# A hybrid decoder layer: the conditioning tiles beside the projections of four heads instead of six

## The chip, the cores and the metric

The kernel runs on one core of one Trainium2 chip. The metric is the device time of one execution in microseconds (us); it stands beside the span, which is the time between the first and the last instruction that the profiler recorded.

## The reference

One layer, 512 tokens of width 2048, all in float32. A conditioning vector `c` gives six vectors of 2048 (shift, scale and gate for the mixing and for the MLP) by a product with `w_ada` (2048 x 12288, 100 MB). The mixing has 8 heads of HGRN2 and 8 heads of Gated DeltaNet in parallel, each with four projections of 128 columns of `w_in`.

```
c_act = silu(c)
mod = c_act @ w_ada + b_ada
sh_m, sc_m, gt_m, sh_f, sc_f, gt_f = split(mod, 6)
h = rmsnorm(x, pre_mix_norm) * (1 + sc_m) + sh_m
proj = h @ w_in
o = concat(hgrn2_group(proj[:4096]), gdn_group(proj[4096:]))
x = x + gt_m * rmsnorm(o @ w_out, post_mix_norm)
h = rmsnorm(x, pre_ffn_norm) * (1 + sc_f) + sh_f
x = x + gt_f * rmsnorm(square(relu(h @ w_ff1)) @ w_ff2, post_ffn_norm)
```

`w_in` is 2048 x 8208; a row takes 32,832 bytes, a row of `w_ada` 49,152.

## The kernel before

Activations stand with the feature dimension on the partitions: `hH` and `hL` are the 16 tiles of `h`, split into a rounded part and a rest so that three fast products of rounded numbers give the accuracy of float32. Every weight tile is split the same way.

**Weights.** `WeightStream` walks a list `plan` of weight tiles, each `raw` tile 128 partitions x 1024 floats (512 KB). One fetch (`get`) of tile *i* first issues the load of tile *i*+3 on SyncE's queue (L66), then splits tile *i*+1: ScalarE casts it to `wh` (L81), VectorE subtracts to `wl` (L83). There are three `raw` buffers, two `wh` and two `wl`. SyncE works in order: a load whose buffer isn't free holds back every load behind it.

**Projections.** A start stage (to 294 us in the profile) computes shift and scale of the mixing, `h`, and the projections of heads zero and one. Then a loop over heads two to seven projects each head's eight blocks of 128 columns (four of each group). A block is two tiles, `("in1", column, half)`, so a head has 16 fetches and the loop 96. A tile is read as 1024 pieces of 128 floats, one from each of 1024 rows of `w_in`. The products go to `pj` in PSUM, 24 matmuls per fetch. In the trace the tiles of a head are `raw32` to `raw47` for head two, and so on to `raw96` to `raw111` for head six and `raw112` to `raw127` for head seven. (The profile leaves the numbers out and writes `raw`; all of them are issued at L66.)

**Recurrences.** Between these matmuls stand those of the recurrences of the heads before (names like `p`, `pa`, `po`). Which matmul stands where is set when the program is written, by a clock of modelled costs; TensorE's and SyncE's order is then fixed. ScalarE, VectorE and GpSimd get their order from a scheduler. All engines work in order.

**The conditioning of later stages.** The three segments that are wanted after the mixing (scale and shift of the MLP, gate of the mixing: segments 4, 3 and 2 of `w_ada`, in this order) are computed beside the projections of heads two to seven, by the generator `ada_rest`. A segment has 4 column blocks of 512, a block 16 rows per partition: 3 x 4 x 16 = 192 steps. A step is one load of 128 x 512 floats (256 KB, `ada`, L302), issued six steps ahead into seven buffers; one scaling on ScalarE by an element of `c` per partition (L320), which is placed behind the last cast of a weight tile; and one add on GpSimd into the block's accumulator `aacc` (L322). Five steps after a block's last step follows its end: for segments 4 and 3 sums over the partitions on TensorE (`pca`); for segment 2 a load of a row of `b_ada` (`bgt`, L1151) and an add of it on GpSimd (L1152). After the projections those four accumulators are summed on TensorE (`pgw`) and multiplied with `post_mix_norm` (`wpost`, L1287).

Each fetch calls `on_get`, which runs as many steps as are due: after *n* fetches of the loop, 192 *n* / `total` steps. What is left of the generator after the last projection is run then (`for _ in steps: pass`).

The output projection (`pout`), the residual and norms, and the MLP (`pf`, `pg`) follow; the MLP takes more than half of the span.

Of the kernel before, what the change touches and what calls it, by code (L numbers as in the profile page):

```python
# [15 lines left out]
P = 128  # L16
# [92 lines left out]
def hybrid_layer_kernel(  # L109
# [30 lines left out]
    def wrow(W, r, nb):  # L140
        return W[r : r + 256, nb * 512 : (nb + 1) * 512].rearrange("(k p) n -> p k n", p=P)
# [14 lines left out]
    plan = []  # L156
# [15 lines left out]
    for nbs in ((0,), (0, 1), (2,), (3,)):  # L172
        for i, r in enumerate(OUT_PAIRS):
            for nb in nbs:
                e = (("out", r, nb), wrow(Wo, r * P, nb))
# [1005 lines left out]

    steps = ada_rest()
    pace = {"on": False, "n": 0, "done": 0}
    total = sum(1 for e in plan if e[0][0] == "in1") - 12

    def on_get():
        if not pace["on"]:
            return
        pace["n"] += 1
        while pace["done"] * total < pace["n"] * 192:  # L1190
            pace["done"] += 1
            next(steps, None)
# [130 lines left out]
    with ExitStack() as st:  # L1323
# [42 lines left out]
        for nb in range(1, 4):  # L1366
            ps4 = [bank("pj", f"pout{nb}_{tok}") for tok in range(3)] + [bank("sg", f"pout{nb}_3")]
            n = 8 if nb < 3 else 8 - NLAST
# [25 lines left out]
        for kt in range(KT):  # L1394
# [10 lines left out]
            if kt % 3 < 2:  # L1405
                nc.scalar.activation(out=h2H[:, kt, :], in_=ht, func=AF.Identity, bias=shf[:, kt : kt + 1])
                nc.vector.scalar_tensor_tensor(out=h2L[:, kt, :], in0=ht, scalar=shf[:, kt : kt + 1],
                                               in1=h2H[:, kt, :].bitcast(F32), op0=ALU.add, op1=ALU.subtract)
# [188 lines left out]
```

## Time and profile before

| | us |
|---|---|
| median of 3 runs | 2716.35 |
| lowest, highest | 2715.49, 2717.22 |
| the profiled execution | 2714.78 |
| its span | 2713.1 |
| busy: TensorE (PE) | 2563.6 |
| busy: VectorE (DVE) | 1440.6 |
| busy: ScalarE (ACT) | 1016.4 |
| busy: GpSimd (POOL) | 569.9 |
| projections of heads two to seven, first and last `pj` matmul | 294 to 1096 |

The page of the profile gives the busy time of each engine, the span in 40 slices (a digit is a busy share in tenths; PEclk is the granted clock of TensorE in tenths), the DMA queues, and groups of instructions. Other views are tables of time windows (per engine the busy time and, in brackets, the number of instructions, then granted clock, busy share of the 16 DMA engines and GB/s), waits (who waited for whom: us in total, times, longest), and one tile's instructions (shortest / median / longest in ns, first and last start). SPq is SyncE's queue. In the DMA view of a window, a row of a load has the number issued, the size of one and the median us from issue to landing. "Busy" of TensorE is a time in which matmuls are in flight, not a measure of its rate.

### The profile page before, as it was taken

How to read it: one execution, taken by the hardware profiler on the slowest of the kernel's cores; microseconds unless marked ns; L12 is line 12 of the kernel's file. 1: busy time of each engine (PE TensorE's matmuls, PEld its weight loads, DVE VectorE, ACT ScalarE, POOL GpSimd, SP SyncE). 2: the span in 40 equal slices, each digit the busy share in tenths (PEclk: the TensorE clock that was granted, in tenths of full speed). 3: DMA queues.
4: the chain of work that ended last, by engine and by line, in shares of the span. 5: the costliest groups of instructions: out<-in, count | busy, mean ns of one | idle time of the engine just before them, and what ended most of it. 6: DMA issues, size and time to landing. Idle time of an engine off the chain costs nothing.

```text
span 2713.1 us, 34048 instructions
## 1 busy us (share of the span) xinstructions
PE 2563.6 (94%) x12987; PEld 2080.2 (77%) x12987; DVE 1440.6 (53%) x2265; ACT 1016.4 (37%) x1675; POOL 569.9 (21%) x496
## 2 busy tenths in 40 slices
PE   5889999999997789999999999999999999999997
PEld 3667777777775567788788888888888888888886
DVE  7997868776865366634533343334333344334346
ACT  5543554454543242433533233332233223322233
POOL 4560344544444340000100000000000000000003
PEclk8999999999998899999999999999999999999999
DMA  9974885778899985445233333333333333332342
GB/s 280 283 186 73 133 138 128 151 138 153 139 138 103 98 135 79 143 129 186 90 117 109 118 112 115 111 114 111 112 117 111 115 110 116 105 101 93 101 171 109
DMA packets 335938, 350.65 MB, mean 129 GB/s; under 512 B 17191, under 2 KB 255001, under 8 KB 334621
## 3 DMA queue, kind: packets, MB, share of 16 engines
q1 hardware_dynamic: 335578, 348.42, 53.8%
q8 instruction: 102, 1.67, 0.2%
q14 instruction: 62, 0.51, 0.1%
q10 hardware_dynamic: 196, 0.06, 0.0%
HBM read 340.01 MB, written 8.40 MB: 128 GB/s over the span
## 4 chain that ended last, share of the span: by engine, by line
PE 65%; DVE 5%; DMA 3%; issue 2%; POOL 1%; ACT 1%; SPq 0%; DVEq 0%; ACTq 0%; POOLq 0%
PE pf L203 25%; PE pg L203 25%; PE pj L203 7%; PE pout L203 6%; DMA raw<-in_w_in_dram 2%; DVE wl L83 1%; PE pa L203 1%; POOL y L1521 0%; POOL aacc L322 0%; DVE x2r L1539 0%; DVE uc L912 0%; DVE utmp L910 0%; PE p L203 0%; DVE zkT L364 0%; PE pz L203 0%
## 5 line engine op out<-in xcount | busy, mean ns | idle before, releaser
L83 DVE TENSOR_TENSOR wl<-raw,wh 128x1024 fp32r<-128x1024 f32 x418 | 525.4, 1258 | 827.3 <-ACT wh L81 821.0
L81 ACT CAST wh<-raw 128x1024 fp32r<-128x1024 f32 x424 | 445.9, 1052 | 1216.5 <-PE pg L203 477.9
L203 PE MATMUL pf<-h2L,wh 128*128 128x512 f32 x1024 | 399.2, 390 | 0.0
L203 PE MATMUL pf<-h2H,wh 128*128 128x512 f32 x1024 | 399.2, 390 | 0.0
L203 PE MATMUL pf<-h2H,wl 128*128 128x512 f32 x1024 | 398.9, 390 | 0.0
L203 PE MATMUL pg<-wh,gL 128*128 128x512 f32 x992 | 385.9, 389 | 0.0
L203 PE MATMUL pg<-wl,gH 128*128 128x512 f32 x992 | 385.9, 389 | 0.0
L203 PE MATMUL pg<-wh,gH 128*128 128x512 f32 x992 | 385.9, 389 | 0.0
L203 PE MATMUL pj<-hH,wh 128*128 128x512 f32 x768 | 328.9, 428 | 7.3 <-ACT wh L81 7.3
L322 POOL TENSOR_TENSOR aacc<-ada,aacc 128x512 f32<-128x512 f32 x180 | 268.5, 1492 | 256.7 <-ACT ada L320 222.7
L203 PE MATMUL pj<-hH,wl 128*128 128x512 f32 x768 | 308.2, 401 | 6.9 <-DVE wl L83 6.9
L203 PE MATMUL pj<-hL,wh 128*128 128x512 f32 x768 | 306.7, 399 | 0.0
L322 POOL TENSOR_TENSOR gacc<-ada,gacc 128x512 f32<-128x512 f32 x64 | 83.2, 1300 | 940.6 <-ACT ada L320 940.6
L203 PEld LDWEIGHTS pf<-h2L,wh 128*128 128x128 f32 x1024 | 192.5, 188 | 39.9
L203 PEld LDWEIGHTS pf<-h2H,wh 128*128 128x128 f32 x1024 | 192.5, 188 | 39.8
L203 PEld LDWEIGHTS pf<-h2H,wl 128*128 128x128 f32 x1024 | 192.4, 188 | 39.8
L203 PEld LDWEIGHTS pg<-wl,gH 128*128 128x128 f32 x992 | 186.2, 188 | 38.7
L203 PEld LDWEIGHTS pg<-wh,gH 128*128 128x128 f32 x992 | 186.2, 188 | 38.6
L203 PEld LDWEIGHTS pg<-wh,gL 128*128 128x128 f32 x992 | 186.2, 188 | 38.6
L1482 DVE TENSOR_TENSOR y<-pg,y 128x512 f32<-128x512 f32 x232 | 154.6, 687 | 70.7 <-PE pg L203 70.7
L203 PEld LDWEIGHTS pj<-hH,wl 128*128 128x128 f32 x768 | 148.0, 193 | 44.0 <-DVE wl L83 10.5
L203 PEld LDWEIGHTS pj<-hH,wh 128*128 128x128 f32 x768 | 148.5, 193 | 37.8 <-ACT wh L81 8.7
(411 smaller groups left out, 3346.3 us busy)
## 6 DMA issues: line engine op xcount, KB each, us to landing
raw<-in_w_ff_dram SPq DMA_DIRECT2D x256, 512.0 KB, 3.7
ada<-in_w_ada_dram SPq DMA_DIRECT2D x256, 256.0 KB, 7.9
raw<-in_w_in_dram SPq DMA_DIRECT2D x96, 512.0 KB, 9.4
adas<-in_w_ada_dram SPq DMA_DIRECT2D x128, 256.0 KB, 5.4
raw<-in_w_out_dram SPq DMA_DIRECT2D x40, 512.0 KB, 3.8
raw<-in_w_in_dram SPq DMA_DIRECT2D x40, 256.0 KB, 4.2
raw<-in_w_in_dram SPq DMA_DIRECT2D x48, 128.0 KB, 5.3
xo<-in_x_dram SPq DMA_DIRECT2D x8, 512.0 KB, 8.7
```

The lines of the kernel that those rows point to most:

```text
L81: self.cast = self.nc.scalar.copy(out=h, in_=raw).ins
L83: eng.tensor_tensor(out=lo, in0=raw, in1=h.bitcast(F32), op=ALU.subtract)
L203: nc.tensor.matmul(ps, lhsT=lhsT, rhs=rhs, start=start, stop=stop)
L322: nc.gpsimd.tensor_tensor(out=acc, in0=a, in1=acc, op=ALU.add)
L1482: nc.vector.tensor_tensor(out=dst, in0=ps4[tok], in1=dst, op=ALU.add)
```

## The change

`total`, the number of fetches over which the 192 steps are spread, was the number of `in1` tiles less 12, 84: the steps ran from head two into the fourth fetch of head seven. It becomes the number of tiles of heads two to five, 64. The count of fetches stops at `total`, so the steps that `on_get` runs stop at 192 exactly; the end of the last block of segment 2, which one further call would have run, is now left to the loop after the last projection.

```diff
     steps = ada_rest()
     pace = {"on": False, "n": 0, "done": 0}
-    total = sum(1 for e in plan if e[0][0] == "in1") - 12
+    total = sum(1 for e in plan if e[0][0] == "in1" and e[0][1] % 1024 < 6 * P)
 
     def on_get():
         if not pace["on"]:
             return
-        pace["n"] += 1
+        pace["n"] = min(pace["n"] + 1, total)
         while pace["done"] * total < pace["n"] * 192:
             pace["done"] += 1
             next(steps, None)
```

SyncE's queue, from the third weight tile of head six on. An `ada` name has the first column of its block in `w_ada` and the row of the step: `ada4608_5` is segment 2, second block, row 5; `ada5632` is the fourth and last block. Before:

```order
L66 DMA raw98_7785<-in_w_in_dram 128x8x128
L302 DMA ada4608_5_7791<-in_w_ada_dram 128x512
L302 DMA ada4608_6_7794<-in_w_ada_dram 128x512
L302 DMA ada4608_7_7798<-in_w_ada_dram 128x512
L66 DMA raw99_7877<-in_w_in_dram 128x8x128
L302 DMA ada4608_8_7883<-in_w_ada_dram 128x512
L302 DMA ada4608_9_7887<-in_w_ada_dram 128x512
L1151 DMA bgt0_7891<-in_b_ada_dram 1x512
L66 DMA raw100_7940<-in_w_in_dram 128x8x128
```

Now, the same queue from the second-last tile of head five on (`E6` is a load for head six's recurrence that stands at this place in both):

```order
L66 DMA raw95_7745<-in_w_in_dram 128x8x128
L302 DMA ada5632_9_7751<-in_w_ada_dram 128x512
L1151 DMA bgt2_7755<-in_b_ada_dram 1x512
L302 DMA ada5632_10_7758<-in_w_ada_dram 128x512
L302 DMA ada5632_11_7762<-in_w_ada_dram 128x512
L66 DMA raw96_7809<-in_w_in_dram 128x8x128
L302 DMA ada5632_12_7815<-in_w_ada_dram 128x512
L302 DMA ada5632_13_7819<-in_w_ada_dram 128x512
L302 DMA ada5632_14_7823<-in_w_ada_dram 128x512
L840 DMA E6_7852<-gd_184 128x4x128
L66 DMA raw97_7903<-in_w_in_dram 128x8x128
L302 DMA ada5632_15_7909<-in_w_ada_dram 128x512
```

The last conditioning load now stands before `raw98`; from there to `raw127` the queue holds weight tiles and head seven's `E7` alone. In heads two to five each weight load has three conditioning loads behind it, where it had two or three.

The load of the last row of `b_ada`, `bgt3`, stood between `raw119` and `raw120` of head seven; now it is issued after `raw130`, a tile of `w_out`, right ahead of the four loads of `post_mix_norm`.

ScalarE's queue in head four, at the casts of two weight tiles (`thvT4`, `zvT4`, `upvT4`: the convolution of head four's values). Before:

```order
L81 CAST wh71_6058<-raw71_5899 128x1024
L360 COPY upvT4_6043<-pj6656_5898 128x512
L362 ACTIVATE zvT4_6046<-pj6656_5898,convT_98 128x512
L320 ACTIVATE ada6656_7_5792<-ada6656_7_5792,c2_99 128x512
L320 ACTIVATE ada6656_8_5905<-ada6656_8_5905,c2_99 128x512
L320 ACTIVATE ada6656_9_5909<-ada6656_9_5909,c2_99 128x512
L368 ACTIVATE thvT4_6051<-zvT4_6046 128x512
```

Now:

```order
L81 CAST wh71_6176<-raw71_6030 128x1024
L360 COPY upvT4_6161<-pj6656_6029 128x512
L362 ACTIVATE zvT4_6164<-pj6656_6029,convT_98 128x512
L320 ACTIVATE ada7680_2_6040<-ada7680_2_6040,c2_99 128x512
L320 ACTIVATE ada7680_3_6044<-ada7680_3_6044,c2_99 128x512
L320 ACTIVATE ada7680_4_6085<-ada7680_4_6085,c2_99 128x512
L368 ACTIVATE thvT4_6169<-zvT4_6164 128x512
```

At such a fetch with three steps nothing changes but the step's number (27 steps on); a fetch with two gets a third scaling ahead of the copies behind it.

## The prediction

> **What bounds the kernel now.** I read the page first, for which engine fills the span and where it does not.
>
> ```profile
> span 2713.1 us, 34048 instructions
> PE 2563.6 (94%) x12987; PEld 2080.2 (77%) x12987; DVE 1440.6 (53%) x2265; ACT 1016.4 (37%) x1675; POOL 569.9 (21%) x496
> PE   5889999999997789999999999999999999999997
> PEclk8999999999998899999999999999999999999999
> DMA  9974885778899985445233333333333333332342
> ```
>
> TensorE is the bound nearly everywhere. The exception inside the kernel is slices 13 and 14 (one slice is 67.8 us, so about 814 to 950 us): TensorE falls to seven and eight tenths, its granted clock falls with it, and the DMA engines are at nine. That lies inside the stretch that the change touches, the projections of heads two to seven. So the second view is a table of windows, one per head. The heads' bounds are the starts of their first `pj` matmul; the last two rows cut head seven where the conditioning ends, and the row of 1100 is the output projection.
>
> ```profile
> core 0: us, PE busy (x) PEld busy (x) DVE busy (x) ACT busy (x) POOL busy (x), PEclk, DMA share, GB/s
> 294.00:434.00 140.00, 131.73 (x895) 105.64 (x894) 106.13 (x238) 66.41 (x143) 66.71 (x52) 0.96 0.81 141
> 434.00:564.00 130.00, 122.26 (x832) 97.63 (x832) 96.52 (x187) 60.46 (x125) 62.96 (x49) 0.99 0.68 144
> 564.00:690.00 126.00, 118.57 (x755) 95.94 (x754) 86.29 (x166) 58.25 (x122) 57.98 (x45) 0.99 0.83 150
> 690.00:810.00 120.00, 114.74 (x723) 90.46 (x722) 85.85 (x151) 58.45 (x113) 57.09 (x45) 1.00 0.88 138
> 810.00:984.00 174.00, 130.52 (x700) 101.28 (x698) 80.76 (x154) 58.90 (x115) 56.38 (x46) 0.87 0.99 109
> 984.00:1020.00 36.00, 34.23 (x192) 27.94 (x191) 31.43 (x49) 19.57 (x47) 22.95 (x18) 1.00 0.70 119
> 1020.00:1097.00 77.00, 76.91 (x492) 61.38 (x492) 44.27 (x102) 20.82 (x39) 4.22 (x5) 1.00 0.52 82
> 1100.00:1140.00 40.00, 38.98 (x204) 30.72 (x202) 28.72 (x54) 19.13 (x39) 2.39 (x2) 1.00 0.39 120
> ```
>
> Head six takes 174 us where head five takes 120 and head seven 36 + 77 = 113. Its DMA engines are busy all the time (0.99) and yet move less, 109 GB/s against 138 to 150. So they are the bound there, and something makes their work dearer. The DMA view of that stretch (787 to 960 us, from its loads' first data on) and one row of the waits in it:
>
> ```profile
> q1 hardware_dynamic: 21607, 17.42, 101.1%
> ada<-in_w_ada_dram SPq DMA_DIRECT2D x37, 256.0 KB, 15.7
> raw<-in_w_in_dram SPq DMA_DIRECT2D x16, 512.0 KB, 20.3
> ACT wh L81 <- DMA raw<-in_w_in_dram: 79.0, 12, 10.8
> ```
>
> 16 weight loads and 37 conditioning loads fill 101% of 173 us, 175 us of all 16 engines' time. ScalarE's casts wait 79.0 us for weights; TensorE's own waits carry other names, because ScalarE works in order and its other copies stand behind a cast that waits. What makes the weights dear is not their size, which is that of every head. I take it to belong to head six's loads, for it comes and goes with them. SyncE's issue of a weight load, which grows when the DMA engines don't keep up:
>
> ```profile
> L66 SPq DMA_DIRECT2D raw<-in_w_in_dram x17: 378/379/1979, 661.7 to 782.8; - x17
> L66 SPq DMA_DIRECT2D raw<-in_w_in_dram x16: 1656/3310/4324, 794.2 to 956.4; - x16
> ```
>
> The load issued at 782.8 is `raw96`, head six's first, and the one at 956.4 is `raw112`, head seven's first. From 960 us on the DMA has recovered, while the conditioning goes on:
>
> ```profile
> DMA  9998998894999657985568896547998897888655
> GB/s 70 56 88 132 271 276 195 220 125 96 337 198 152 122 129 236 243 146 68 71 199 226 111 60 110 109 129 263 297 207 119 122 134 78 103 168 173 174 66 48
> ```
>
> (960 to 1010 us in 40 slices, with 11 conditioning loads and 7 weight loads issued.) It is no accident of one execution: 50 us lost once in a while would show between the runs, and they lie within 1.73 us of each other.
>
> **The change part by part.** A conditioning step is one load of 256 KB, one scaling on ScalarE and one add on GpSimd. Before, 84 fetches carry 192 steps, 16/7 each: 64 x 16/7 = 146 steps in heads two to five, 46 in heads six and seven. Now the first 64 fetches carry 3 each. So 46 steps move ahead, 11.5 more per head in heads two to five; nothing is added or removed in number.
>
> *Head six loses its conditioning loads.* Price of one load in engine time: the fastest slice above moves 337 GB/s, so 0.78 us for 256 KB; the output projection's loads, in rows as long, run at 120 / 0.39 = 308 GB/s, 0.85 us. The slow stretch itself never exceeds 217 GB/s in a slice, 1.21 us, but weights move in that slice too. So 37 x 0.78 = 29 us to 37 x 1.21 = 45 us. I take 29, from the slice most nearly of conditioning alone.
>
> ```profile
> GB/s 91 54 150 117 93 156 69 148 81 95 124 45 113 107 69 217 46 109 101 53 195 67 80 93 62 164 84 41 141 72 76 161 81 140 101 122 83 46 113 97
> ```
>
> It counts whole on the path: 174 - 29 = 145 us is still more than the 120 us of head five, so head six remains paced by its weights, 175 - 29 = 146 us over 16, some 9.1 us each.
>
> The Trainium skill, page "DMA: Bandwidth & Descriptors", section "Latency and other measured facts", has a rule on this: when each partition reads at a large power-of-two row pitch, copies fell from 207 GB/s to 103. The pitch of w_ada between partitions is 768 KiB; at 207 GB/s, an estimate from that page, the 37 loads would be worth 47 us instead of 29. The slice of 337 GB/s disagrees, so I keep the row.
>
> *Heads two to five get 46 more steps.* On ScalarE 0.72 us each and on GpSimd 1.49 us, from these rows:
>
> ```profile
> L320 ACT ACTIVATE ada<-ada,c x244: 705/718/732, 299.6 to 2344.8; 128x512 f32<-128x512 f32 x122
> L322 POOL TENSOR_TENSOR aacc<-ada,aacc 128x512 f32<-128x512 f32 x180 | 268.5, 1492 | 256.7 <-ACT ada L320 222.7
> SPq L302 <- POOL aacc L322: 66.9, 46, 7.2
> PE py L203 <- DVE Ud L928: 1.6, 1, 1.6
> ```
>
> Per head that is 8 us on ScalarE (58 to 66 of 120 to 140 now) and 17 us on GpSimd (57 to 67 now): both stay under 65%. It lies beside TensorE, except where a copy for a recurrence stands behind a third scaling instead of a second. TensorE is idle 8.27 + 7.74 + 7.43 + 5.26 = 28.7 us in the four heads now. If all of it came from the 146 steps, 46 more would cost 28.7 x 46 / 146 = 9.0 us, and the stretch without steps (0.09 us idle in 77) speaks for that; the waits that are named there, as the last row above (660 to 790 us), are for VectorE in the recurrences, which speaks for nothing. Ends 0 and 9, I take the middle, 4.5.
>
> *SyncE's queue.* Each fetch issues its weight load and then three conditioning loads; the last waits for GpSimd's add two steps back, and the next weight load stands behind it. The third row above is that wait over 564 to 790 us: 1.5 us each, 7.2 at most, against a weight load that lands three fetches (over 22 us) before its matmuls. Cover: 22 less the landing of 11.1 us below, about 11 us; nothing charged. If it went, each fetch would wait for the excess.
>
> ```profile
> DMA to landing us min/median/max: 8.5/11.1/17.7
> ```
>
> *DMA share in heads two to five.* 11.5 loads x 0.85 = 9.8 us per head: 0.81 becomes 0.88, 0.68 becomes 0.76, 0.83 becomes 0.91, 0.88 becomes 0.96. Below one, so nothing charged; head five is near, see the rivals.
>
> *The bias rows.* Three of four `bgt` loads move with their steps into head five, the fourth to the end of the projections. GpSimd waits for them in order:
>
> ```profile
> POOL aacc L1152 <- DMA bgt<-in_b_ada_dram: 45.2, 3, 24.4
> POOL aacc L1152 <- DMA bgt<-in_b_ada_dram: 2.1, 1, 2.1
> L203 PE MATMUL pgw<-aacc,ones x8: 592/592/595, 1098.1 to 1101.2; 128*128 128x512 f32 x8
> L1287 SPq DMA_DIRECT2D wpost<-in_post_mix_norm_dram x4: 327/375/462, 1085.1 to 1101.1; - x4
> ```
>
> 43.1 us of that wait fell in the slow stretch and 2.1 us (the second row, 980 to 1120 us) after it. In head five I take 2 us in all on the path; ends 0, and 30 if three loads each held TensorE for a 10 us landing. The fourth is issued just ahead of `wpost` at 1085; even at 5.4 us to land (the slowest `wpost`) and 1.3 us for the add it is ready by 1092, 6 us before `pgw` at 1098. Cover: those 6 us; without them the wait's excess would go straight to the output projection.
>
> *The column sums and the order.* The sums of segments four and three come earlier in TensorE's order, the same instructions; no cost.
>
> Sum: -29 + 4.5 + 2 = -22.5 us. The profiled execution took 2714.78 us around its span of 2713.1, and the median of the runs is 1.57 us above it: 2716.35 - 22.5 = 2694 us. A measurement here tells about 0.2%, 5.4 us, from no change.
>
> **The rivals.**
>
> *Head six runs like its neighbours.* If dear weights need the conditioning beside them, head six falls from 174 to 120 us: -54 + 6.5 = -47.5, 2669 us. For it: no head is dear without conditioning beside it. Against: heads three to five have the same mixture and are not dear.
>
> *The dearness goes with segment two's columns of w_ada*, steps 144 to 183, loaded in the same stretch. They would then be in head five: 37 / 3 = 12.3 fetches at 175 / 16 + 0.7 x 0.85 = 11.5 us each instead of 7.5, +49; head six -54; +6.5 for the rest: 2718 us, no change. Against it: the recovery at 960 us comes with segment two still loading.
>
> *Slower: the DMA fills up.* If the stretch is dear because the queue overflowed at a share near one, heads four (0.91) and five (0.96) overflow now: 16 x 11.5 = 184 us each instead of 126 and 120, +122; head six without steps -54; 2784 us. It decides from a share of 1.0. Against it: the first 106 us of the projections already ran at 0.87, and moved 145 GB/s:
>
> ```profile
> 294.00:400.00 106.00, 99.57 (x653) 79.78 (x652) 78.00 (x166) 53.16 (x111) 52.41 (x41) 0.97 0.87 145
> ```
>
> *Slower: GpSimd's adds hold VectorE.* 46 adds come beside a VectorE that is 68 to 76% busy, instead of 46% in head six. At worst each holds VectorE for its 1.35 us median, 62 us on TensorE's path: 2716 - 29 + 62 = 2749. Against it, from the page: 418 splits of the same shape
>
> ```profile
> L83 DVE TENSOR_TENSOR wl<-raw,wh 128x1024 fp32r<-128x1024 f32 x418 | 525.4, 1258 | 827.3 <-ACT wh L81 821.0
> L83 DVE TENSOR_TENSOR wl<-raw,wh x17: 1208/1225/2306, 660.4 to 780.1; 128x1024 fp32r<-128x1024 f32 x17
> L322 POOL TENSOR_TENSOR aacc<-ada,aacc x180: 1252/1351/2375, 300.4 to 1009.5; 128x512 f32<-128x512 f32 x180
> ```
>
> average 50 ns over their shortest, though single ones take 2306. The Trainium skill, page "SBUF — State Buffer", section "SBUF: two separate sides", says the two engines share a port pair as an exclusive lock held for a whole instruction; the 2306 ns agrees, the average says it is rare.
>
> *Nothing arrives.* Head six could be set by the bias waits (43.1 us of GpSimd), which only move: 2716. Against it: the DMA share is 1.01 right through them.
>
> **How the numbers follow.** The forecast 0.60; head six like its neighbours 0.16; segment two 0.07; overflow 0.08; the lock 0.04; nothing 0.05. Faster by over 0.2%: 0.60 + 0.16 = 0.76. Within: 0.07 + 0.05 = 0.12. Slower: 0.12. The forecast's own range is 2678 (45 us gained, little paid back) to 2704 (29 gained; 9 and 8 paid). The range that leaves out the two slower cases and the fringe of the others is 2660 to 2716.
>
> **What would show it.** Right: in the table by head, head six near 145 us, still with DMA near 1.0, GB/s nearer 60 and ScalarE still waiting for `raw`; heads two to five longer by some 5 us together; head seven and all after it the same. Head six near 120 us, or a slow stretch in heads four or five with DMA at 1.0 and low GB/s, would show one of the rivals. The forecast is wrong if the dearness does not stay with head six, or if the 29 us reappear as TensorE idle in heads two to five.

## The result, and the profile after

The changed kernel takes 2731.56 us (median of 4 runs, 2730.58 to 2733.49), the kernel before 2716.78 beside it (4 runs, 2715.49 to 2718.59). The ratio is 1.0057, with a 95% interval of 1.0044 to 1.0069: 0.6% slower, where 2694 us was forecast. The profiled execution of the changed kernel took 2730.58 us around its span. Its page, the rows that answer to those of before:

```profile
span 2728.8 us, 34055 instructions
PE 2573.1 (94%) x12987; PEld 2090.9 (77%) x12987; DVE 1445.9 (53%) x2265; ACT 1017.7 (37%) x1675; POOL 575.0 (21%) x496
PE   5889999898988899999999999999999999999997
PEclk9999999999989899999999999999999999999999
DMA  9964886687979986345333333333333333333353
```

TensorE has the same 12987 matmuls and is busy 9.5 us longer for them; the row PEclk is lower in several slices. Where one slice was at seven tenths before, several are now at eight. The table of windows, one row per head from two to seven, has the columns of the prediction's table:

```profile
293.00:440.00 147.00, 132.55 (x892) 106.05 (x892) 114.06 (x241) 72.47 (x151) 82.03 (x61) 0.95 0.82 154
440.00:577.00 137.00, 125.88 (x849) 99.74 (x848) 101.43 (x187) 67.34 (x136) 80.26 (x59) 0.96 0.72 156
577.00:712.00 135.00, 122.13 (x754) 98.09 (x754) 93.10 (x166) 66.67 (x134) 74.20 (x56) 0.95 0.82 157
712.00:858.00 146.00, 121.32 (x708) 97.07 (x707) 93.84 (x151) 65.95 (x125) 77.77 (x59) 0.91 0.82 137
858.00:1003.00 145.00, 126.32 (x698) 99.61 (x697) 67.45 (x155) 36.13 (x78) 7.82 (x11) 0.89 0.97 65
1003.00:1113.00 110.00, 110.00 (x680) 89.38 (x680) 67.52 (x150) 35.13 (x76) 8.91 (x11) 1.00 0.54 78
```

Head six fell from 174 to 145 us, as forecast, with the DMA engines still full at 65 GB/s. The loss is in heads two to five: 516 us became 565. TensorE's idle time there (each row's length less its busy time) grew from 28.7 to 63.1 us, and its busy time from 487.3 to 501.9 for the same matmuls, the granted clock being 0.91 to 0.96 in place of 0.96 to 1.00. So 34 of the 49 us are waits and 15 a slower clock beside them.

All per-head times below run from the start of a head's first `pj` matmul to that of the next head's (head seven's to the end of its last `pj` matmul), in us, each from one profiled execution; "2-5" is the sum of heads two to five. Before head two and after head seven the kernels agree within 4 us unless something else is said. A single head is sure to some 4 us only: head two takes 139.4 us in the kernel before and 136.2 in `split67` below, head three 130.5 and 134.9, though neither head is changed there; the sum of heads two to five differs by 1.2.

| kernel | 2 | 3 | 4 | 5 | 2-5 | 6 | 7 |
|---|---|---|---|---|---|---|---|
| before | 139.4 | 130.5 | 126.0 | 120.0 | 515.9 | 173.7 | 113.0 |
| after | 147.1 | 137.4 | 135.1 | 145.8 | 565.4 | 144.7 | 110.1 |
| difference | +7.7 | +6.9 | +9.1 | +25.8 | +49.5 | -29.0 | -2.9 |

Four waits stand out in heads two to five. In order: SyncE's wait in front of a conditioning load, before (294 to 810 us) and after (293 to 858 us); then from head five after (712 to 858 us) ScalarE's wait for conditioning tiles, TensorE's wait for one copy of VectorE (`hat`), and its wait for one copy of ScalarE (`vn`).

```profile
SPq L302 <- POOL aacc L322: 129.2, 94, 7.2
...
SPq L302 <- POOL aacc L322: 276.0, 118, 12.2
ACT ada L320 <- DMA ada<-in_w_ada_dram: 21.1, 8, 9.9
PE hpo L203 <- DVE hat L1118: 9.1, 1, 9.1
PE p L203 <- ACT vn L1015: 7.3, 1, 7.3
```

None of the last three is in head five of before as a loss: its wait for `hat` was 0.4 us, and no wait of ScalarE for a conditioning tile is among its largest. The last two are 16.4 of the 24.7 us that TensorE is idle in head five after. Each is a suspect, and so is whatever lengthens every head by 7 to 9 us. SyncE's own waits rose by less than the first two rows say, for its wait in front of a weight load, for VectorE's `wl`, fell from 91.5 to 36.2 us.

### The profile page after: what moved, and what is told of

Same layout as the page of the kernel before. It is cut to its first block, busy times and chain, and to the rows that moved or that the text cites. A ratio compares the mean times of both kernels' runs of the same rounds, so it can differ in the third digit from the quotient of the medians.

```text
span 2728.8 us, 34055 instructions
## 1 busy us (share of the span) xinstructions
PE 2573.1 (94%) x12987; PEld 2090.9 (77%) x12987; DVE 1445.9 (53%) x2265; ACT 1017.7 (37%) x1675; POOL 575.0 (21%) x496
## 4 chain that ended last, share of the span: by engine, by line
PE 62%; DMA 4%; DVE 1%; POOL 1%; ACT 1%; issue 0%; DVEq 0%; ACTq 0%; POOLq 0%; SPq 0%
PE pf L203 25%; PE pg L203 25%; PE pout L203 6%; PE pj L203 4%; DMA raw<-in_w_in_dram 4%; POOL y L1521 0%; DVE x2r L1539 0%; PE pa L203 0%; DVE wl L83 0%; ACT wh L81 0%; PE p L203 0%; PE hpo L203 0%; DVE h2L L1407 0%; PE po L203 0%; DMA wpost<-in_post_mix_norm_dram 0%
## 5 line engine op out<-in xcount | busy, mean ns | idle before, releaser
L320 ACT ACTIVATE ada<-ada,c 128x512 f32<-128x512 f32 x244 | 166.1, 717 | 52.9 <-DMA ada<-in_w_ada_dram 51.9
```

Of the source, the lines that this page charges most:

```text
L320: nc.scalar.activation(out=dst[:, s], in_=a[:, s], func=AF.Copy, scale=c2[:, r0 + r : r0 + r + 1])
```

## The experiments

Ratios are to the kernel before, in runs on the same chip (its median there 2713 to 2714 us).

### Do the costly loads belong to head six?

`swap36`: the kernel before, in which heads three and six read each other's columns of w_in.

```diff
-            plan.append((("in1", col, hf), w128(Wi, col, hf)))
+            src = col + {3: 3, 6: -3}.get(col % 1024 // P, 0) * P
+            plan.append((("in1", col, hf), w128(Wi, src, hf)))
```

> The kernel before, but head three's projections read the columns of w_in that belong to head six, and head six's read head three's (so both heads compute with the other's weights). If the dear weight loads belong to those columns, head three becomes the slow head: about 130 + 50 = 180 us with the DMA share near 1.0 and about 100 GB/s, and head six falls from 174 to about 125 us; the total stays within 10 us of the kernel before. If they belong to the time or to the conditioning columns loaded then, head six stays near 174 us and head three near 130.

Measured: 2702.66 us, ratio 0.9958 (0.9942 to 0.9974). The long head is now the third, 169.7 us at a DMA share of 1.00, and the sixth takes 123.5. Packets of 512 bytes averaged 146 ns in the third head's loads and 49 in the sixth's; before it was 50 and 146. (The total, expected within 10 us, fell by 11.) So the dearness goes with these columns, wherever they are loaded and whatever is loaded beside them. Why these columns are slow is not shown.

### What do the loads, the scalings and the adds of a step cost in heads two to five?

`noload` is the changed kernel without the 192 conditioning loads (the steps scale a constant tile), `noadd` the changed kernel without GpSimd's 180 adds. Each leaves out a part of the modulation.

```diff
 noload
-                    tiles[(s2, c2_, r2)] = ada_load(...)
+                    tiles[(s2, c2_, r2)] = ada_pool_.tile([P, T], F32, tag="ada", ...)
 noadd
-        if not first:
+        if not first and add:
             nc.gpsimd.tensor_tensor(out=acc, in0=a, in1=acc, op=ALU.add)
```

> The changed kernel without the 192 conditioning loads: each step scales a constant tile instead, into the same seven buffers, and adds as before. Heads two to five take 565 us in the changed kernel (294 to 858), 516 in the kernel before. Buffer theory (loads are issued late, because their buffers come back from GpSimd late, and ScalarE then waits for them in order with the weight casts behind): heads two to five fall to about 516 us or less. Port theory (46 more adds on GpSimd lengthen VectorE's instructions and with them TensorE's waits): they stay near 555 us, and VectorE's busy time in them stays near 402 us (375 in the kernel before). Head six about 145 us in both; total 2680 or 2722 us.

> The changed kernel without GpSimd's 180 adds of the steps (the accumulators keep their first row); loads and scalings stay, and the buffers come back after the scaling. Port theory: VectorE's busy time in heads two to five falls well below the 402 us of the changed kernel, towards 340 (46 adds more cost it 27 us, 180 would cost some 100), and the heads take 500 us or less. Scaling theory (the third scaling on ScalarE stands ahead of the recurrences' copies): the heads stay near 550 us. Buffer theory: 520 us or less too, but with VectorE's busy time changed little. Total about 2665 us (port), 2720 (scaling), 2685 (buffer).

Measured: without loads 2720.08 us, ratio 1.0022 (1.0012 to 1.0031); without adds 2665.15 us, ratio 0.9817 (0.9801 to 0.9834). Leaving the loads out brings 8.6 us in heads two to five, all of it in head five (145.8 to 136.5). Leaving the adds out brings 63 us: the four heads fall to 127.3, 122.1, 122.1 and 130.8. The first two of these in the table of windows:

```profile
294.00:422.00 128.00, 127.11 (x895) 102.39 (x894) 91.50 (x245) 72.95 (x154) 13.85 (x18) 1.00 0.96 179
422.00:544.00 122.00, 121.00 (x850) 97.15 (x850) 76.02 (x183) 67.65 (x137) 9.80 (x13) 1.00 0.80 177
```

TensorE is idle 1.9 us in them where it was idle 25.6, at a clock of 1.00, and VectorE's busy time has fallen by 48 us though it runs the same instructions. How, these instructions show. Three rows each (count, busy us, mean ns) over heads two to five, of before and then of after: a product of two tiles in SBUF, a convolution's step in SBUF, and a copy out of PSUM.

```profile
L1078 DVE TENSOR_TENSOR KS<-KS,tot 128x256 f32<-128x256 f32 x27 | 18.9, 699 | 0.0
L364 DVE SCALAR_TENSOR_TENSOR zkT<-upkT,convT,zkT 128x512 f32<-128x512 f32 x12 | 14.4, 1196 | 0.6 <-ACT zkT L362 0.3
L1032 DVE COPY at<-po 128x128 f32<-128x128 f32 x22 | 6.2, 284 | 0.4
...
L1078 DVE TENSOR_TENSOR KS<-KS,tot 128x256 f32<-128x256 f32 x27 | 25.4, 940 | 0.0
L364 DVE SCALAR_TENSOR_TENSOR zkT<-upkT,convT,zkT 128x512 f32<-128x512 f32 x12 | 13.9, 1156 | 0.1
L1032 DVE COPY at<-po 128x128 f32<-128x128 f32 x22 | 6.2, 283 | 0.7 <-PE po L203 0.5
```

and the same three without adds (`noadd`):

```profile
L1078 DVE TENSOR_TENSOR KS<-KS,tot 128x256 f32<-128x256 f32 x28 | 12.8, 457 | 0.0
L364 DVE SCALAR_TENSOR_TENSOR zkT<-upkT,convT,zkT 128x512 f32<-128x512 f32 x12 | 9.0, 747 | 0.9 <-ACT zkT L362 0.7
L1032 DVE COPY at<-po 128x128 f32<-128x128 f32 x22 | 6.3, 285 | 2.9 <-PE po L203 2.6
```

The product takes 457, 699 or 940 ns in the mean as no, 137 or 180 adds stand in these heads, the convolution's step 747, 1196 or 1156; the copy out of PSUM takes 283 to 285 whatever GpSimd does. So an add holds up VectorE instructions that work in SBUF. It does so now and then: the product's median is some 420 ns in all three kernels, and the mean grows by those that are held up, to 1.5 us at most. In sum VectorE's busy time in the four heads falls by 97.3 us when 180 adds go, 0.54 us for each.

Then the square is closed by the same edit of the kernel before (`bnoadd`), and the loads and adds are taken out together, scalings left alone, after (`scaleonly`) and before (`bscaleonly`); `tiny` cuts the scalings of `scaleonly`, all but the first of each block, from 512 columns to 8. All four leave out a part of the modulation.

```diff
 scaleonly, bscaleonly (and no loads, as noload)
-            ada_pool(tiles.pop((seg, cb, r)), 512, r, 1, acc, r == 0, ws.cast)
+            a = tiles.pop((seg, cb, r))
+            with tc.issue_after(ws.cast):
+                nc.scalar.activation(out=c3(acc if r == 0 else a), in_=fixed, func=AF.Copy, scale=c2[:, r : r + 1])
 tiny
+                    nc.scalar.activation(out=a[:, :8], in_=ones[:, :8], func=AF.Copy, scale=c2[:, r : r + 1])
```

> The kernel before without GpSimd's 180 adds of the conditioning steps (the loads and ScalarE's scalings stay, the modulation is wrong). With the same edit of the changed kernel this makes a square: order before or after, with or without adds. Theory A (an add holds up VectorE's reads of SBUF): heads two to five lose about 0.34 us for each of their 146 adds, 516 becomes 465 to 480, head seven loses 5, head six, which its loads pace, keeps 174 within 3; total about 2660, ratio 0.980. Then the 46 moved steps without their adds cost 502 less 470, some 30 us, which would have to be found among loads, scalings and order. Theory B (the adds cost nothing by themselves, only at the density of 46 to 48 a head in the changed kernel): heads two to five stay over 500, total 2700, ratio 0.995.

> The changed kernel without the 192 conditioning loads and without the adds: only ScalarE's scalings are left of the steps, of a constant tile. Theory A: against the kernel without adds only (2665 us) it gains what late loads cost in head five there, 6 to 9 us: 2657, ratio 0.978, heads two to four unchanged within 2 us. Rival: with adds gone the loads are free as well, 2665. If head five still takes over 125 us without loads and adds (120 before with both), what is left there is the order of instructions.

> The kernel before with ScalarE's scalings alone (no conditioning loads, no adds; the modulation is wrong). Against the same edit of the changed kernel (heads two to five 127, 122, 119, 121: 489 us) it shows what moving 46 scalings costs with all else gone. If the loads of the kernel before were hidden in heads two to five, these stay at 476 as without adds alone, and 13 us of the 49 belong to scalings or to the order of instructions; head six falls from 171 to 142 to 146 with its 37 loads gone. Rival: heads two to five fall to about 465, and the loads cost 10 us there before the change too.

> The changed kernel without conditioning loads and adds, and with each scaling cut from 512 columns to 8, so that the order of instructions stays as it is and ScalarE's time for them goes. If the rest of 13 us in heads four and five belongs to the order in which VectorE's instructions stand (the copy of the third output block behind some 10 us of other work): head five stays at 119 to 122, total 2645 to 2655. If it is ScalarE's time: head five falls to 112 to 114, and the total to 2635 to 2645.

Measured:

| what is left of a step | before's order, 2-5 | after's order, 2-5 | difference | ratio, before's / after's order |
|---|---|---|---|---|
| load, scaling, add | 515.9 | 565.4 | +49.5 | 1 / 1.0057 |
| load, scaling | 475.9 | 502.3 | +26.4 | 0.9841 / 0.9817 |
| scaling | 476.1 | 489.3 | +13.2 | 0.9737 / 0.9783 |
| scaling of 8 columns | not run | 487.4 | | - / 0.9768 |

Down the differences: 23 of the 49.5 us are adds, 13 loads, 13 what stays when both are gone. These shares hold for taking the adds out first: with the adds still there, taking the loads out of the changed kernel brought 8.6 us and not 13, and the kernel before wasn't run without loads alone. In the order before, with adds gone, the loads cost heads two to five nothing (475.9 against 476.1). Without adds the change would have been no loss: the ratio is 0.9817 (0.9801 to 0.9834) with it and 0.9841 (0.9826 to 0.9856) without it, a gain of 0.2% at the edge of what the runs tell.

An add costs VectorE much the same before and after: 71.2 us of busy time for 137 adds and 97.3 for 180, 0.52 and 0.54 us each. The heads pay more for each: 40.0 us for the 137 adds of before, 0.29 us each; 63.1 us for the 180 of after, 0.35 each. If 137 of these cost 40.0 as before, the 43 on top cost 0.54 each. Whether the price rises because the adds are denser or because the order around them is another is not shown. Head four fell by 2.7 us when the loads were taken out as well, a little more than expected; head five came down to 120.9, against 112.6 in the order before. ScalarE's scalings, cut to 8 columns, bring only 2 of the last 13 us, which is hardly clear of what a head varies by.

### Is it GpSimd's being busy, or what it reads?

`memadd` puts three memsets of GpSimd in the place of each add of the changed kernel; `vecsteps` makes a whole step one instruction of VectorE.

```diff
 memadd
-            nc.gpsimd.tensor_tensor(out=acc, in0=a, in1=acc, op=ALU.add)
+            for _ in range(3):
+                nc.gpsimd.memset(a, 0.0)
 vecsteps
-            ada_pool(tiles.pop((seg, cb, r)), 512, r, 1, acc, r == 0, ws.cast)
+            with tc.issue_after(ws.cast):
+                ada_vector(tiles.pop((seg, cb, r)), 512, r, 1, acc, r == 0)
```

> The changed kernel with three memsets of GpSimd (128x512 each, of the tile just scaled) in place of each add, about 1.5 to 1.8 us of GpSimd together; the modulation is wrong. If an add costs because GpSimd reads and writes SBUF beside VectorE's reads: VectorE's KS product stays near 460 to 600 ns (457 without adds, 940 with) and heads two to five near 502 to 520, total 2665 to 2685, ratio 0.982 to 0.990. If any work of GpSimd costs the same for its time: KS at 900 and more, total as the changed kernel, 2725 to 2735.

> The changed kernel with each conditioning step as one instruction of VectorE (tile times factor plus accumulator) in place of ScalarE's scaling and GpSimd's add; the output is the same sum. Theory A: VectorE pays some 0.75 us openly (what such a 128x512 instruction took without adds beside it) where an add took 0.56 us from it by lengthening its instructions, so 192 x 0.19 = 36 us more of VectorE, about 60 in 100 of it in the end: 2745 to 2755, ratio 1.010 to 1.015, and VectorE's own instructions as short as without adds (the KS product 450 to 500 ns instead of 940). Theory B (the adds cost by GpSimd's queue, by what waits behind them, or by ScalarE's scalings): 2680 to 2700, ratio 0.990.

Measured: with memsets 2653.13 us, ratio 0.9775 (0.976 to 0.979). That is less than expected, because the memsets also replace adds ahead of head two, which starts 25 us earlier; the heads are what compares. GpSimd is as busy as in the changed kernel, in head three for instance 76 us of 123 (the last of the busy columns of this row), and VectorE hardly feels it:

```profile
396.00:519.00 123.00, 121.54 (x851) 97.19 (x850) 77.12 (x180) 67.67 (x136) 76.24 (x149) 1.00 0.77 174
L1079 DVE TENSOR_TENSOR KS<-KS,tot 128x256 f32<-128x256 f32 x28 | 12.8, 456 | 0.0
```

(The line is one further down than in the other kernels.) Heads two to five take 513.4 us, 52 less than after and 11 more than without adds. So of the 63 us that the adds cost, 52 come from what an add does and a memset doesn't, which is to read two tiles of SBUF (a memset writes one, as an add does), and 11 from GpSimd's being occupied, 8 of these in head five. The memsets are not quite harmless to VectorE: the recurrence's products and the convolutions' steps, with two inputs in SBUF, keep their time, but a few instructions with one input there grow, as these of `memadd`, which take 542 and 378 ns without adds:

```profile
L400 DVE TENSOR_SCALAR f<-hth,hga,hgb 128x512 f32<-128x512 f32 x5 | 3.5, 705 | 0.2 <-ACT hth L397 0.2
L907 DVE COPY uc<-im 128x64 f32<-128x64 f32 x5 | 3.7, 741 | 0.0
```

A step on VectorE took 2927.65 us, ratio 1.0791 (1.0775 to 1.0807), and both theories missed. VectorE, which works in order, now waits for the conditioning tiles itself (first row, 296 to 1058 us; the second is of 294 to 850 us):

```profile
DVE aacc L311 <- DMA ada<-in_w_ada_dram: 267.7, 51, 14.9
L1078 DVE TENSOR_TENSOR KS<-KS,tot 128x256 f32<-128x256 f32 x20 | 8.3, 417 | 0.0
```

Its own products are short (417 ns), as the theory of adds says; what the step's arithmetic costs there can't be read behind 268 us of waits.

### Is the rest the order of instructions?

The change leaves VectorE's queue in another order all along, and in head five the third copy of an HGRN output block (`hat`, L1118) has come to stand behind the work on the next head's solve. `order5` is the changed kernel with that solve's second part traced 1.5 us later by the planner's clock, which puts the copies in front; the output is the same.

```diff
-        yield 3.0
+        yield 4.5 if h == 5 else 3.0
         Ap = mt("Ap", f"Ap{h}", 1, (P, NCH, P))
```

> The changed kernel with the second part of one solve, that of the fifth place, traced 1.5 us later by the planner's clock (a yield of 4.5 in place of 3.0), which puts VectorE's third and fourth copies of the HGRN output ahead of that solve's eleven instructions in head five; the output is the same. If the order is what costs head five its 9 us wait of TensorE for the copy: the wait is gone, head five 145.8 becomes 136 to 140, total 2720 to 2726, 0.2 to 0.4% under the changed kernel. Rival: VectorE is full there, and TensorE waits as long for something else in head five: no change within 3 us.

Measured: head five 137.3 us in place of 145.8, as expected, and the wait is gone. TensorE is idle 17.7 us there, 24.7 after. But the total is 2729.32 us, ratio 1.0056 (1.0044 to 1.0069), that of the changed kernel: head six takes 150.4 us in place of 144.7.

```profile
711.00:848.00 137.00, 119.30 (x684) 94.17 (x683) 94.58 (x148) 62.80 (x119) 75.83 (x58) 0.94 0.84 140
848.00:998.00 150.00, 125.22 (x710) 98.12 (x710) 67.07 (x154) 37.45 (x83) 8.77 (x12) 0.91 0.97 67
```

Heads five and six together gain only 2.8 us. Head six is paced by its loads, which start in head five; a shorter head five gives them less time ahead. `raw96`, the first of them, is issued 29.5 us ahead of head six after and 23.5 us here, and from its issue to the start of head seven it is 174.2 and 173.8 us. So the order does cost head five its 8.5 us, as part of the 49.5, but little of the total. Heads three and four also keep 1 to 4 us each in `tiny`. In head four all of TensorE's idle time there is one wait for VectorE's `at` (L830, 3.1 us); which rows of the order cause it was not tried.

### Where should the steps stand?

`pause6` spreads the steps over heads two to five and seven and leaves head six without; `total96` spreads them evenly over all 96 half fetches. Both give the same output as before.

```diff
 pause6 (against the changed kernel)
-    total = sum(1 for e in plan if e[0][0] == "in1" and e[0][1] % 1024 < 6 * P)
+    total = sum(1 for e in plan if e[0][0] == "in1") - 16
...
+        key = plan[ws.ng - 1][0]
+        if key[0] == "in1" and key[1] % 1024 == 6 * P:
+            return
 total96 (against the kernel before)
-    total = sum(1 for e in plan if e[0][0] == "in1") - 12
+    total = sum(1 for e in plan if e[0][0] == "in1")
```

> The steps spread evenly over the fetches of heads two to five and seven, none in head six: 192 / 80 = 2.4 per fetch instead of 16/7 = 2.29 (before) or 3 (changed). If the loss in the changed kernel grows with the number of steps per fetch: heads two to five about 516 + 49 x 0.11 / 0.71 = 524 us, head six near 145 us, head seven about 3 us longer than before; 2716 - 29 + 8 + 3 = 2698 us, faster than both. If three steps in one fetch are harmless until something tips over, the same or better, 2690. If head six's gain came from what stands in heads two to five and not from its own loads, near 2716.

> The kernel before with its steps spread evenly over all 96 half fetches of heads two to seven, two to a fetch: each of the heads two to six gives up 4.6 steps and head seven takes 23 more. By the prices found so far (0.55 us a step added in head seven, 0.78 us a step in head six, 0.4 to 0.9 us in heads two to five): 12.7 - 3.6 - 18 x 0.65 = -3 us, 2711, ratio 0.999, between 0.995 and 1.003. Theory C (a step costs the same 0.6 us wherever it stands, so that only the total counts): no change within 0.2%.

Measured: `pause6` 2720.23 us, ratio 1.0029 (1.0018 to 1.004), where 2698 was expected: head six 152.5, but head seven 129.3, 16 us more for its 29 further steps, and heads two to five 529.8 (its profiled execution lies 4 us above the median). `total96` 2714.07 us, ratio 1.0003 (0.9993 to 1.0012): head six 165.0, head seven 121.5, heads two to five 511.7. So no place is free: 0.78 us a step there (29.0 / 37), 0.56 in head seven (16.3 / 29), 1.08 in heads two to five (49.5 / 46) at the density of the change. These prices don't carry over from kernel to kernel, though: in heads two to five `pause6` pays 13.9 us for 7 more steps, and `total96` gains 4.2 for 18 fewer. None of the spreadings tried gained.

### Moving the costly columns instead

These kernels keep the steps where they are and change which head is projected where; the output is that of the reference. `split67` and `split36` exchange only the delta-rule part of head six, with that of head seven or three, so that half the costly columns stay in the sixth place; `swap36c` exchanges heads three and six whole; `split67a` is the change on top of `split67`.

```diff
+    def gm(h):
+        return {3: 6, 6: 3}.get(h, h)
...
-            plan.append((("in1", col, hf), w128(Wi, col, hf)))
+            plan.append((("in1", col, hf), w128(Wi, wcol(col), hf)))
...
-            d["k"] = conv_silu(u, 8 + h, "kT", f"kT{h}", 2)
+            d["k"] = conv_silu(u, 8 + gm(h), "kT", f"kT{h}", 2)
...
-        yield from finish_head(f"g{h}", 8 + h, d["osb"], d["sso"], nwh[:, 1:2], d["g"], d["rqs"])
+        yield from finish_head(f"g{h}", 8 + gm(h), d["osb"], d["sso"], nwh[:, 1:2], d["g"], d["rqs"])
```

(`wcol` maps a delta-rule column of head h to that of head gm(h); the decays, factors and the order of waiting for finished heads go through `gm` alike.)

> The kernel before with the delta-rule parts of heads six and seven exchanged (columns, convolution taps, decays, rows of the output), so that the sixth place projects head seven's delta-rule columns and head six's HGRN columns and the seventh place the other two; the output is the same. The costly loads of head six (about 130 ns a 512-byte packet in the mean against 60) are then half in each place. If these columns are costly wherever they stand and only their bunching makes the DMA engines the bound: the sixth place has 174 less 8 fetch pairs' worth, about 45 us, and is paced by TensorE again at 122 to 130, the seventh place 113 to 122; total 2655 to 2680, ratio 0.978 to 0.988. If loads are costly because of the place in the program, or slow each other down so that nothing is averaged: no change, 2713, or the two places together still 280 or more.

> The change on top of that exchange. The theory that the change gained its 29 us in head six only because the DMA engines were the bound there, and pays about 1 us for each of 46 steps in heads two to five: now head six gives back only what a step costs beside TensorE, 37 x 0.3 to 0.55 = 11 to 20 us, and heads two to five still pay 49; so 25 to 35 us slower than the exchange alone, 2690 to 2705 in all. If the step is worth 0.78 us in head six by other ways than the loads, the change costs 16 us here as well.

> The kernel before with the delta-rule parts of heads three and six exchanged, so that half of head six's costly columns are projected in the third place, whose DMA share was 0.68; the output is the same. From the exchange of six and seven (150 and 130 us for the two, half of the costly columns each): sixth place about 148, third place 135 to 142, 304 becomes 283 to 290, total 2692 to 2700, ratio 0.992 to 0.996. If a run of three costly columns is a stall in either place: no better than the exchange with seven, ratio 0.998.

> The kernel before with heads three and six exchanged whole (columns, taps, decays, bounds, rows of the output): the output is the same. As the run that exchanged the columns alone: third place 170, sixth place 124, total 2700 to 2705, ratio 0.9958 within 0.0015. If that run was fast for its wrong data and not for the place of the columns: 2713.

| kernel | us | ratio (95%) | 2 | 3 | 4 | 5 | 6 | 7 |
|---|---|---|---|---|---|---|---|---|
| split67 | 2708.23 | 0.9985 (0.9976 to 0.9993) | 136.2 | 134.9 | 126.0 | 120.0 | 149.5 | 129.8 |
| split67a | 2727.14 | 1.0054 (1.0042 to 1.0067) | 147.7 | 137.4 | 135.1 | 138.8 | 134.6 | 120.8 |
| split36 | 2685.13 | 0.9895 (0.9881 to 0.9908) | 139.3 | 136.7 | 125.9 | 120.0 | 136.9 | 116.7 |
| swap36c | 2702.93 | 0.9958 (0.9945 to 0.997) | 139.4 | 169.4 | 127.1 | 120.0 | 123.6 | 111.8 |

`split67` gained much less than expected: head seven paid for what head six saved. In the sixth place the three costly HGRN columns follow each other, and the DMA share there is still 0.96. The change on top of it (`split67a`) costs 18.9 us: 41.9 more in heads two to five, and head six now gives back 14.9 in place of 29.0, which is what the theory had expected (11 to 20), and head seven 9.0, which it had not; so the cost is under the 25 to 35 us expected. `split36` is the best version of this study, 28 us under the kernel before and 7 under the range expected. Its third and sixth place:

```profile
431.00:568.00 137.00, 126.34 (x836) 100.56 (x836) 97.02 (x189) 60.91 (x126) 63.37 (x49) 0.96 0.88 143
814.00:951.00 137.00, 120.44 (x696) 94.29 (x695) 83.22 (x154) 56.64 (x113) 54.94 (x43) 0.94 0.92 121
```

The third place, whose DMA share was 0.68, takes half of the costly columns for 6 us; the sixth loses 37. Neither is full any more (0.88 and 0.92). Why head three takes the columns so much better than head seven, whose DMA share before was only 0.58, is not shown. One difference is in the order of loads: the blocks of a head are loaded as three of the delta rule, three of HGRN2 and one of each, so that in `split67` the costly blocks at the end of the sixth place are followed at once by those of the seventh.

## Why the prediction was wrong, point by point

- *The bound in head six, and that it belongs to head six's loads.* Right. `swap36` moved it with the columns.
- *Head six loses 37 loads at 0.78 us, 174 to 145 us, still paced by its weights.* Right to the microsecond, 144.7 us, which is partly luck, for the two prices weighed there gave 129 and 145. The price holds in another pair of kernels too: with the adds gone, leaving out the loads brings head six of the order before from 170.5 to 142.4 us, 0.76 us for each of 37. In the DMA view of after, over the same stretch of its loads (835 to 975 us), the 16 weight loads alone fill the engines, and the casts still wait for them in head six:

```profile
q1 hardware_dynamic: 16263, 8.95, 100.8%
raw<-in_w_in_dram SPq DMA_DIRECT2D x16, 512.0 KB, 24.0
ACT wh L81 <- DMA raw<-in_w_in_dram: 73.9, 12, 10.9
```

- *46 more steps in heads two to five, 4.5 us between ends of 0 and 9.* This is the step that failed: it measured 49.5 us. It scaled TensorE's idle time by the number of steps, as if each step cost the same, and it counted ScalarE's and GpSimd's time as lying beside TensorE. Without adds the order before leaves TensorE 0.6 us idle in heads two to five (475.4 busy of 476), so nearly all of the 28.7 us idle that was scaled came from adds; the waits named there, for VectorE in the recurrences, were the trace of that, where the prediction said that they spoke for nothing. And the cost did not follow the count. Of the 34 us of added idle time, 19 are there without adds too (19.8 us in `noadd` against 0.6): they belong to loads and order, and the idle time that was scaled held next to nothing of either. The idle time that goes with the adds rose from 28.1 to 43.3 us for 137 and 180 of them, where the count alone gives 36.9. And the granted clock was lower beside the waits, 15 us that the scaling of idle time left out altogether. These rows of the kernel before without adds (`bnoadd`) are the evidence for the idle time:

```profile
295.00:422.00 127.00, 126.65 (x894) 101.91 (x893) 91.48 (x244) 66.11 (x140) 12.49 (x18) 1.00 0.90 158
422.00:542.00 120.00, 120.00 (x834) 96.83 (x833) 76.06 (x183) 60.86 (x126) 9.66 (x13) 1.00 0.73 155
542.00:658.00 116.00, 115.76 (x752) 94.33 (x751) 69.18 (x164) 57.98 (x122) 7.80 (x11) 1.00 0.88 160
658.00:771.00 113.00, 113.00 (x727) 91.19 (x725) 66.85 (x152) 58.92 (x113) 9.77 (x11) 1.00 0.90 148
```

- *The rival of the adds, chance 0.04.* It named the right mechanism for 23 of the 49.5 us and a price of 62 us at worst. It was set aside on the mean of 418 splits, 50 ns over their shortest. That mean was taken over the whole kernel, and the adds of the stretch end at 1009 us; the same splits average 1373 ns in heads two to five of before and 1237 without adds, and the products of the recurrence, which were not looked at, 699 against 457. The rule of the Trainium skill (page "SBUF — State Buffer", section "SBUF: two separate sides"), that the two engines take turns on one port pair for whole instructions, agrees with the products in SBUF that grow. The same page says more, which the prediction did not use (section "Who interferes with whom"): a VectorE instruction with two inputs in SBUF contends with a GpSimd instruction that reads SBUF, and not with one that only writes it. The memsets agree: as much of GpSimd's time left the product at 456 ns. By that rule the list of what an add can hold up (the splits, the products of both recurrences, the convolutions) and what it can't (copies out of PSUM) could have been drawn up from the names in the trace. The price measured is less than a whole add: 0.52 to 0.54 us of VectorE's time and 0.29 to 0.54 us of the path, for an add of 1.5 us.
- *SyncE's queue and the DMA share, nothing charged.* Wrong by 9 to 13 us, most of it in head five. SyncE's wait in front of conditioning loads doubled (129 to 276 us) and head five's conditioning tiles came late. The DMA share did not rise as worked out (0.82 in head five in place of 0.96), since the head grew longer. The record points at the DMA engines more than at the queue: without adds, when buffers come free early, ScalarE still waited 29 us for tiles in head five. What the prediction did not look at is the end of that head, where the last conditioning loads stand behind `raw96`, the first of the costly loads. The first of them was issued at 829.7 us, and its tile was there at 845.7, 16 us later, where 10.1 is the head's median. ScalarE had waited 9.9 us for it, the copy `vn` stood right behind that scaling, and TensorE waited the 7.3 us for `vn`. In `split67a`, where head six's first blocks are not the costly ones, that wait is 3.0 us and head five takes 138.8.
- *The bias rows, 2 us.* GpSimd waited 8.7 us for two of them in head five, 2 us forecast on the path; what of it is in the 49.5 was not separated. The longer wait, 7.1 us until 824.6, is followed by the end of a 6.8 us wait of SyncE for GpSimd at 828.2, right ahead of `raw96` and the late loads; so it may have a part in the 7.3 us above. The fourth, at the end, was hidden as forecast: what follows head seven takes 1615.9 us, 1616.1 before.
- *The order: no cost.* Wrong by up to 13 us in heads two to five, the part that stays when loads and adds are gone. All of TensorE's idle time that is left in head five then is its wait for `hat`, 6.9 us (9.1 in the changed kernel). `order5` took this wait away and shortened head five by 8.5 us, at the cost of 5.7 in head six. The prediction compared queues of SyncE and ScalarE, and never VectorE's, whose order had shifted throughout.
- *The other rivals.* Head six did not run like its neighbours (144.7 us, not 120). The dearness did not go with segment two's columns of w_ada, as `swap36` shows. No stretch of heads four and five overflowed as that rival had it: 135.1 and 145.8 us, not 184 each.
- *The sum.* 49.5 - 29.0 - 2.9 = +17.6 us by heads, less some 2 us around them: the spans differ by 15.7. What was forecast to show the prediction wrong, the 29 us that reappear as TensorE idle in heads two to five, is what happened, with 34 idle and 15 of clock.

## What to carry to other kernels

Price a step that is moved by all the engines it disturbs, not by its own engine's free time: take a stretch of the same work with and without such steps, and compare the durations of the other engines' instructions there, group by group, not a mean over the kernel. A step that costs 0.8 us where its loads are the bound may cost 1.1 us where no engine is full: here 23 of 49.5 us because it lengthens work of another engine that TensorE waits for, and the rest by late loads and by the order of instructions. When one stretch is bound by loads, bringing half of them to another stretch can gain more than moving other work away (28 us here, with no more work), but the share of busy DMA alone does not tell which stretch: head three at 0.68 gave these 28 us, head seven at 0.58 gave 5.

## What was not expected of the hardware

- That the order of a traced program can give back what it takes: the wait of 9 us that `order5` removed from head five came back as 5.7 us of head six, which its loads pace.
- An add of GpSimd over two tiles in SBUF (128x512, 1.5 us) cost VectorE 0.54 us of longer instructions in the mean, doubling a product that takes 457 ns without adds, at 180 adds in 565 us. Three memsets in its place (529 ns each) left the recurrence's products and the convolutions' steps, with two inputs in SBUF, as they were, and lengthened a few instructions with one (542 to 705 ns, 378 to 741).
- The weight loads of one eighth of w_in's columns take 2 to 3 times as long as the others (512-byte packets 146 ns in the mean, 50 to 83 in heads two to five and seven), in the third place of the program as in the sixth, and with or without conditioning loads beside them. Nothing that was tried says why.
